# A hybrid attention and gMLP block: the output gate of the attention in pairs of products, one activation table, and the second branch's blocks beside two heads

## The chip, the core and the metric

The kernel runs on one core of one Trainium2 chip. It is written by hand in the Tile language: the program names tiles, pools and engines, and a scheduler orders the instructions of each engine. The metric is the device time of one execution in microseconds (us), here the median of three runs: 1114.92 us (1113.07, 1114.92 and 1116.30). Beside them stands one execution that the hardware profiler took.

## The reference, cut to what matters

One layer on 1024 tokens of 1024 features, fp32. There are four heads with keys of 128 and values of 256.

```python
h = rmsnorm(x, norm_g) * (1 + scale) + shift
p = h @ w_in                                  # 1024 x 8224
q, k, v, z_gla, ra_f, ra_b, u, vs, z_gmlp, m_gla, m_gmlp = split(p)
log_a = max(log_sigmoid(ra @ alpha_w + alpha_b) / 16, -1.25)      # one for each direction
o = gla(q, k, v, log_a_f) + flip(gla(flip(q), flip(k), flip(v), flip(log_a_b), strict))
o = o * rsqrt(mean(o * o) + eps) * gla_norm_g                     # for each head
y_gla = (o * silu(z_gla)) @ w_br_gla
vs = layernorm(gelu(vs)) * ln_g + ln_b
sg = einsum(gmlp_ws, vs) + gmlp_bs                                # chunks of 128 tokens
y_gmlp = (gelu(u) * sg * silu(z_gmlp)) @ w_br_gmlp
merged = sigmoid(m_gla) * y_gla + sigmoid(m_gmlp) * y_gmlp
return rmsnorm(x + gate * (merged @ w_out), final_g)
```

`gla` is a linear attention with a decay, in chunks of 64 tokens: with b the running sum of log_a inside a chunk, it takes q·exp(b) against k·exp(-b) under a triangular mask, and carries a state of 128x256 from chunk to chunk.

## The kernel before, in words

**Products.** Each fp32 operand is split into a high and a low part of the type fp32r: ACT casts the value to the high part and DVE subtracts that from the value (`split_w`, L174 and L175). A product is then three: high x high, high x low and low x high. `dense_fm` computes one block of 128 output columns for all 1024 tokens: 2 halves x 8 k-blocks x 3 = 48 products of 128x512 (L192 to L194). `dense_v` does the same with tokens on the partitions and 256 columns (L509 to L511).

**Pairs of seven products.** `pair(ba, bb, evac)` computes two such blocks at once. It takes sums of the weights (on POOL) and sums of quarters of h (the tiles T1 to T4, made once), and needs seven products of 12 where the two blocks alone would need eight: 7 x 12 = 84 in place of 96 (L546 to L548). DVE adds the partial results and `evac` takes the four quarters of the result. In the kernel before, the pairs hold the two merge gates (`pair_m`, whose tanh goes to the DRAM tiles `tb_d` and `ta_d`) and u and z_gmlp (`pair_uz`, whose product u·sg·silu(z) goes to `gg_d`).

**Stages.** (1) Load x and the modulation, make h high and low. (2) The vs branch with its layernorm and spatial product. (3) v of heads 0 and 1 and the sums T1 to T4; v goes to DRAM. (4) The pairs. Before the last three of them stand `low_rank_weights` and `residual_gate`, which loads eight tiles `wg` and adds them with factors on DVE (L664). (5) The high halves of h are loaded again, q and k of head 0 are computed, and then the attention runs. (6) The gated output GO is multiplied by w_br_gla, merged, multiplied by w_out, and normalized.

**The attention** has 16 units: for each head the sequence backward half 1, backward half 0, forward half 0, forward half 1 (`SEQ`). `front` of a unit (function `gla_unit`) makes the decay: a product `pm` of ST and RT (L764), then on ACT Abs, Exp and Ln (L766 to L768), a DVE subtraction (L769) and a running sum (L773), Exp for the chunk ends, `qh` and `b` (L783, L789, L791), their products with q and k, and the score product `pm` L797. `body` makes the states: `gla_ops` transposes `kh` and splits `kh` and `qh` (L807 to L817), then for each of four tiles there is a state product `pk` (L821 to L823), a DVE step that decays and adds the state, a cast on ACT and a subtraction on DVE (L844 and L845) that split it, and a product `po` of q with the state, evacuated to `op`. The forward units add the masked scores, the mean square, a power on POOL (L220), a scaling (L917), a transpose (L922) and the product with the gate tile `zg` and with `gn`.

**What fills the units.** The fronts and bodies are issued at a priority raised by 4000, so the scheduler puts the other work of the loop where they leave an engine free. That other work is dense blocks: v of head h+2, and q, k and z of head h+1, while head h runs (z of head 0 before the loop); beside head 3 the loads and splits of the second branch (`load_gg`) and its eight blocks `dense_yb`. `dense_z` computes silu(z) times two, as (1 + tanh(z/2))·z, from a tanh on ACT (L720) and a DVE step (L721); `gn` carries the factor 0.5. Tanh, Ln and the Exps need different activation tables; where ACT goes from one to another, an ACT_TABLE_LOAD stands ahead of the function.

**Queues and pools.** SP issues the weight loads, POOL's queue the loads and stores of v, g and the gates. `ht` is a pool of 30 tiles of 4 KB per partition, `w4` one of 12 such tiles, `w2` one of 16 of 2 KB and `w1` one of 8 of 1 KB. In PSUM there are three `pd`, two `pm`, two `po` and one `pk`.

## Time and profile before

| | before |
| --- | --- |
| median of 3 runs | 1114.92 us (1113.07 to 1116.30) |
| the profiled execution | 1113.34 us, of which the span is 1111.6 us |
| mean granted TensorE clock | 0.987 |
| TensorE (PE) busy | 1068.1 us |
| ACT busy | 462.8 us |
| POOL busy | 231.5 us |
| instructions in the span | 14297 |

The span is the time from the first to the last record of the trace, and it is what the shares refer to. PE is TensorE's product, PEld its weight load, which runs beside it; DVE is VectorE, ACT ScalarE, POOL GpSimd, SP the engine that issues most loads. A matmul's record is longer than what it occupies, since products are pipelined: the duration of one is read from a window that is full of them, by dividing. A group of instructions reads "line engine operation, output <- inputs by the program's names, count | busy us, mean ns of one | idle time of the engine just before them, and what ended most of it". A row of waits reads "who waited <- on whom, for what: total us, count, longest".

### The profile page before, as it was taken

To read this page: it belongs to the slowest core of one execution; us is meant where nothing else is said; L and a number is where in the kernel's file an instruction comes from. 1 tells how busy PE (TensorE), PEld (TensorE's weight loads), DVE (VectorE), ACT (ScalarE), POOL (GpSimd) and SP (SyncE) were. 2 spreads that over 40 slices of the span, in tenths; PEclk is the share of its full clock that TensorE was granted. 3 is DMA by queue.
4 is the path that set the end of the run, shared out by engine and by line. 5 is a ranking of instruction groups with operands and counts; after the bars stand their busy time and mean duration, and the time that the engine had idled before them with its cause. 6 is when DMAs were issued, how large, how long until landed. Compare 5 with 4: busy or idle time off the path is not lost.

```text
span 1111.6 us, 14297 instructions
## 1 busy us (share of the span) xinstructions
PE 1068.1 (96%) x5396; PEld 903.2 (81%) x5396; DVE 669.5 (60%) x1057; ACT 462.8 (42%) x780; POOL 231.5 (21%) x262
## 2 busy tenths in 40 slices
PE   6989999999999999989999979998999999999997
PEld 4768899888787878877898879887878888888886
DVE  5765577347666665664566585557788745664422
ACT  4453234232333333333566563556775515221222
POOL 2210213424334252611000011002002010022410
PEclk9999999999999999999999989998999999999999
DMA  9532235233233323367322115103256357516012
GB/s 360 209 107 88 79 126 198 82 106 112 95 123 104 114 105 105 120 230 277 138 83 89 38 49 179 38 19 133 72 177 216 107 193 241 202 58 232 19 57 95
DMA packets 53143, 143.91 MB, mean 129 GB/s; under 512 B 6895, under 2 KB 15087, under 8 KB 53074
## 3 DMA queue, kind: packets, MB, share of 16 engines
q1 hardware_dynamic: 40898, 102.42, 26.2%
q0 software_dynamic: 12176, 40.58, 10.0%
q8 instruction: 42, 0.69, 0.2%
q14 instruction: 27, 0.22, 0.1%
HBM read 104.18 MB, written 38.80 MB: 129 GB/s over the span
## 4 chain that ended last, share of the span: by engine, by line
PE 82%; DVE 5%; ACT 4%; DMA 2%; issue 2%; POOL 1%; SPq 0%; POOLq 0%; ACTq 0%; DVEq 0%
PE pd L193 7%; PE pd L192 7%; PE pd L194 7%; PE pd L211 4%; PE pd L210 4%; PE pd L212 4%; PE po L546 3%; PE po L547 3%; PE po L548 3%; PE pd L510 3%; PE pd L511 3%; PE pd L509 3%; PE pd L1024 3%; PE pd L1026 3%; PE pd L1025 3%
## 5 line engine op out<-in xcount | busy, mean ns | idle before, releaser
L193 PE MATMUL pd<-hl,wh 128*128 128x512 f32 x256 | 100.3, 392 | 0.0
L192 PE MATMUL pd<-hh,wh 128*128 128x512 f32 x256 | 100.1, 392 | 0.0
L194 PE MATMUL pd<-hh,wl 128*128 128x512 f32 x256 | 100.1, 391 | 0.0
L510 PE MATMUL pd<-tvl,hh 128*128 128x256 f32 (+1 forms) x256 | 74.7, 292 | 2.2 <-DVE tvl L175 2.2
L220 POOL TENSOR_TENSOR r<-ms,nhalf 128x1 f32<-128x1 f32 (+1 forms) x24 | 21.8, 909 | 257.7 <-DVE ms L219 184.5
L509 PE MATMUL pd<-tvh,hh 128*128 128x256 f32 (+1 forms) x256 | 74.4, 293 | 0.3 <-ACT tvh L174 0.3
L511 PE MATMUL pd<-tvh,hl 128*128 128x256 f32 (+1 forms) x256 | 74.6, 292 | 0.0
L175 DVE TENSOR_TENSOR wl<-ws,wh 128x1024 fp32r<-128x1024 f32 x32 | 39.1, 1222 | 30.2 <-ACT wh L174 25.9
L174 ACT CAST wh<-ws 128x1024 fp32r<-128x1024 f32 x32 | 33.6, 1049 | 53.8 <-DMA ws<-in_wf 48.3
L192 PEld LDWEIGHTS pd<-hh,wh 128*128 128x128 f32 x256 | 48.1, 188 | 8.9
L194 PEld LDWEIGHTS pd<-hh,wl 128*128 128x128 f32 x256 | 48.1, 188 | 8.8
L193 PEld LDWEIGHTS pd<-hl,wh 128*128 128x128 f32 x256 | 48.1, 188 | 8.8
L548 PE MATMUL pd<-hh,al 128*128 128x512 f32 x128 | 50.3, 393 | 2.7 <-DVE al L175 2.7
L510 PEld LDWEIGHTS pd<-tvl,hh 128*128 128x128 f32 x256 | 50.0, 195 | 2.9 <-DVE tvl L175 2.7
L546 PE MATMUL pd<-hh,ah 128*128 128x512 f32 x128 | 50.4, 394 | 1.3 <-ACT ah L174 1.3
L193 PE MATMUL pd<-ggl,wh 128*128 128x512 f32 x128 | 50.3, 393 | 1.2 <-DVE ggl L175 1.2
L192 PE MATMUL pd<-ggh,wh 128*128 128x512 f32 x128 | 50.4, 395 | 0.0
L509 PEld LDWEIGHTS pd<-tvh,hh 128*128 128x128 f32 x256 | 49.8, 196 | 0.7 <-ACT tvh L174 0.6
L194 PE MATMUL pd<-ggh,wl 128*128 128x512 f32 x128 | 50.2, 392 | 0.0
L511 PEld LDWEIGHTS pd<-tvh,hl 128*128 128x128 f32 x256 | 50.1, 196 | 0.0
L547 PE MATMUL pd<-hl,ah 128*128 128x512 f32 x128 | 49.9, 390 | 0.0
L1024 PE MATMUL pd<-gh,wh 128*128 128x512 f32 x128 | 49.9, 390 | 0.0
(316 smaller groups left out, 3042.8 us busy)
## 6 DMA issues: line engine op xcount, KB each, us to landing
ws<-in_wf SPq DMA_DIRECT2D x32, 512.0 KB, 3.8
ws<-in_wt SPq DMA_DIRECT2D x22, 512.0 KB, 4.1
wa<-in_wada SPq DMA_DIRECT2D x16, 512.0 KB, 8.8
wa<-in_wf SPq DMA_DIRECT2D x16, 512.0 KB, 3.7
wb<-in_wf SPq DMA_DIRECT2D x16, 512.0 KB, 4.8
xn<-in_x SPq DMA_DIRECT2D x8, 512.0 KB, 8.7
sg_d<-sg POOLq DMA_DIRECT2D x16, 256.0 KB, 2.4
vh_d<-vh SPq DMA_DIRECT2D x32, 128.0 KB, 1.9
```

The lines of the kernel that those rows point to most:

```text
L192: TE.matmul(acc, lhsT=hi[:, k, :], rhs=x.hi(k, half), start=(k == 0), stop=False)
L193: TE.matmul(acc, lhsT=hi[:, k, :], rhs=x.lo(k, half), start=False, stop=False)
L194: TE.matmul(acc, lhsT=lo[:, k, :], rhs=x.hi(k, half), start=False, stop=(k == KC - 1))
L210: TE.matmul(acc, lhsT=xh, rhs=hi[:, k % 2, :], start=(k == 0), stop=False)
L211: TE.matmul(acc, lhsT=xh, rhs=lo[:, k % 2, :], start=False, stop=False)
L509: TE.matmul(acc, lhsT=H.hi_t(k, t), rhs=hi, start=(k == 0), stop=False)
L510: TE.matmul(acc, lhsT=H.hi_t(k, t), rhs=lo, start=False, stop=False)
L511: TE.matmul(acc, lhsT=H.lo_t(k, t), rhs=hi, start=False, stop=(k == KC - 1))
L546: TE.matmul(acc, lhsT=a, rhs=xh(k), start=(first and k == 0), stop=False, skip_group_check=not first)
L547: TE.matmul(acc, lhsT=a, rhs=xl(k), start=False, stop=False, skip_group_check=not first)
L548: TE.matmul(acc, lhsT=b, rhs=xh(k), start=False, stop=(k == 3), skip_group_check=not first)
L1024: TE.matmul(acc, lhsT=hi[:, k, :], rhs=GO.hi(k, half), start=(k == 0), stop=False)
```

## The change

Four things change.

- The eight blocks of z are computed as four pairs (`pair_z`) among the other pairs, with the same tanh and DVE step, and stored by POOL in a new DRAM tile `z_d`. `dense_z` is gone; `load_z` loads both tiles of a head from POOL's queue, beside the loads of v. The second `pair_m` on `FB_MA` stands ahead of `low_rank_weights` and `residual_gate` now.
- After the last tanh the activation table that holds both Exp and Ln is loaded by an explicit instruction.
- The filling work is spread anew: head 0 has v of head 2 and q, k of head 1; head 1 has v of head 3 and q, k of heads 2 and 3; head 2 has the second branch's loads and its blocks 0 to 3; head 3 has blocks 4 to 7.
- The tiles `ggf` and `tb` come from the pool `w4` instead of `ht`, and `dense_yb` writes its result into `tb`, so that the tile `yb` is gone.

```diff
@@ -72,6 +72,7 @@
     gg_d = dram("gg_d", [KC, P, T])
     ta_d = dram("ta_d", [KC, P, T])
     tb_d = dram("tb_d", [KC, P, T])
+    z_d = dram("z_d", [KC, P, T])
     b12_d = dram("b12_d", [4, P, 1024])
 
     v_d = [dram(f"v{n}_d", [HEADS, 2, P, 4 * 256]) for n in "hl"]
@@ -631,6 +632,17 @@
         pair(FB_U + 2 * i, FB_U + 2 * i + 1, ev_u)
         pair(FB_ZG + 2 * i, FB_ZG + 2 * i + 1, ev_z)
 
+    def pair_z(i):
+
+        def ev(b, half, acc):
+            z = w2([P, 512], F32, "z")
+            last_tanh[0] = S.activation(z, acc, AF.Tanh, scale=0.5)
+            V.scalar_tensor_tensor(out=z, in0=z, scalar=1.0, in1=acc, op0=ALU.add, op1=ALU.mult)
+            G.dma_start(z_d[2 * i + b, :, half * 512:half * 512 + 512], z)
+        pair(FB_Z + 2 * i, FB_Z + 2 * i + 1, ev)
+
+    last_tanh = [None]
+
     def low_rank_weights():
 
         sa, sr = ht([P, 1024], F32, "sa"), ht([P, 1024], F32R, "sr")
@@ -681,10 +693,18 @@
     pair_uz(2)
     pair_m(FB_MA, ta_d, 0)
     pair_uz(3)
+    pair_m(FB_MA, ta_d, 1)
     low_rank_weights()
     residual_gate()
-    for i in range(1, 4):
-        pair_m(FB_MA, ta_d, i)
+    pair_z(0)
+    pair_m(FB_MA, ta_d, 2)
+    pair_z(1)
+    pair_m(FB_MA, ta_d, 3)
+    pair_z(2)
+    pair_z(3)
+
+    with tc.issue_after(last_tanh[0].ins):
+        S.preload_act_table_set("natural_log_exp_and_others")
 
     for c in range(2):
         hi, lo = H.make(c, 1)
@@ -710,16 +730,10 @@
             S.copy(k_t[h][:, half * 512:half * 512 + 512], acc)
         dense_fm(FB_K + h, H, ev)
 
-    def dense_z(h):
+    def load_z(h):
         for j in range(2):
-            zt = ht([P, T], F32, "zg")
-            z_t[h][j] = zt
-
-            def ev(half, acc):
-                sl = slice(half * 512, half * 512 + 512)
-                S.activation(zt[:, sl], acc, AF.Tanh, scale=0.5)
-                V.scalar_tensor_tensor(out=zt[:, sl], in0=zt[:, sl], scalar=1.0, in1=acc, op0=ALU.add, op1=ALU.mult)
-            dense_fm(FB_Z + h * 2 + j, H, ev)
+            zt = z_t[h][j] = ht([P, T], F32, "zg")
+            G.dma_start(zt, z_d[2 * h + j])
 
     dense_q(0)
     dense_k(0)
@@ -929,7 +943,6 @@
     PRI = 4000
     with tc.high_priority(offset=PRI):
         front(0, 0)
-    dense_z(0)
 
     GG = Act("gg")
 
@@ -937,33 +950,41 @@
         for half in range(2):
             for c in range(KC // 2):
                 hi, lo = GG.make(c, half)
-                g = ht([P, 2, 512], F32, "ggf")
+                g = w4([P, 2, 512], F32, "ggf")
                 for i in range(2):
                     nc.sync.dma_start(g[:, i, :], gg_d[2 * c + i, :, half * 512:half * 512 + 512])
                 split_w(flat(g), flat(hi), flat(lo))
 
     def dense_yb(j):
-        tb, y = ht([P, T], F32, "tb"), ht([P, T], F32, "yb")
+        tb = w4([P, T], F32, "tb")
 
         def ev(half, acc):
-            sl = slice(half * 512, half * 512 + 512)
-            nc.sync.dma_start(tb[:, sl], tb_d[j, :, sl])
-            V.scalar_tensor_tensor(out=y[:, sl], in0=tb[:, sl], scalar=1.0, in1=acc, op0=ALU.add, op1=ALU.mult)
-            G.dma_start(y2_d[j, :, sl], y[:, sl])
+            t = tb[:, half * 512:half * 512 + 512]
+            nc.sync.dma_start(t, tb_d[j, :, half * 512:half * 512 + 512])
+            V.scalar_tensor_tensor(out=t, in0=t, scalar=1.0, in1=acc, op0=ALU.add, op1=ALU.mult)
+            G.dma_start(y2_d[j, :, half * 512:half * 512 + 512], t)
         dense_fm(FB_YB + j, GG, ev)
 
+    def dense_qk(h):
+        dense_q(h)
+        dense_k(h)
+
     for h in range(HEADS):
-        if h + 2 < HEADS:
+        if h < 2:
             dense_v(h + 2, ht)
-        if h + 1 < HEADS:
-            with tc.issue_after(last_pow[0].ins):
+        with tc.issue_after(last_pow[0].ins):
+            load_z(h)
+            if h + 1 < HEADS:
                 load_v(h + 1)
-            dense_q(h + 1)
-            dense_k(h + 1)
-            dense_z(h + 1)
+        if h == 0:
+            dense_qk(1)
+        elif h == 1:
+            dense_qk(2)
+            dense_qk(3)
         else:
-            load_gg()
-            for j in range(KC):
+            if h == 2:
+                load_gg()
+            for j in range(4 * (h - 2), 4 * (h - 2) + 4):
                 dense_yb(j)
         with tc.high_priority(offset=PRI):
             for u in range(4):
```

In the order that results, the engines' rows move as follows. In these rows the line is that of the kernel in question: in the attention a line of the kernel before is 14 lower than its counterpart after (L764 and L778, L822 and L836), and L175 has become L176.

TensorE, right behind the decay product of head 1's first unit, in the kernel before (`pd` with `hh`, `hl` is a product of a dense block of q, k or z; `po` is a product with the state):

```order
L764 MATMUL pm_5819<-RT_4137,ST 128x512
L194 MATMUL pd_4745<-hh_106,wl_4715 128x512
L822 MATMUL po_5024<-sl_5021,qth_4974 128x256
L823 MATMUL po_5024<-sh_5020,qtl_4975 128x256
L192 MATMUL pd_4745<-hh_106,wh_4714 128x512
L193 MATMUL pd_4745<-hl_107,wh_4714 128x512
L194 MATMUL pd_4745<-hh_106,wl_4715 128x512
L192 MATMUL pd_4779<-hh_92,wh_4775 128x512
L193 MATMUL pd_4779<-hl_93,wh_4775 128x512
L194 MATMUL pd_4779<-hh_92,wl_4776 128x512
```

TensorE at the same place in the kernel after (`pk` is a state product):

```order
L778 MATMUL pm_5339<-RT_4687,ST 128x512
L836 MATMUL po_5229<-sl_5226,qth_5184 128x256
L837 MATMUL po_5229<-sh_5225,qtl_5185 128x256
L835 MATMUL pk_5294<-vh_4702,keh_5279 128x256
L836 MATMUL pk_5294<-vl_4703,keh_5279 128x256
L837 MATMUL pk_5294<-vh_4702,kel_5280 128x256
L835 MATMUL po_5289<-sh_5240,qth_5284 128x256
L836 MATMUL po_5289<-sl_5241,qth_5284 128x256
L837 MATMUL po_5289<-sh_5240,qtl_5285 128x256
L835 MATMUL pk_5309<-vh_4702,keh_5279 128x256
```

The dense products that stood between the state products are gone from this place; the state products follow each other.

ACT in the third unit of head 0, before (`vh` is the cast of a block of v that is evacuated):

```order
L766 ACTIVATE e_4936<-pm_4934 128x512
L767 ACTIVATE e_4936<-e_4936 128x512
L768 ACT_TABLE_LOAD
L768 ACTIVATE e_4936<-e_4936 128x512
L500 CAST vh_4486<-pd_4461 128x256
L783 ACT_TABLE_LOAD
L783 ACTIVATE e_842_4946<-c_841_4944 128x8
L789 ACTIVATE qh_4951<-b_4942 128x512
L500 CAST vh_4517<-pd_4492 128x256
L791 ACTIVATE b_4942<-b_4942 128x512
```

ACT in the same unit, after (`sh` is the cast of a state, `q` an evacuation):

```order
L780 ACTIVATE e_5246<-pm_5244 128x512
L781 ACTIVATE e_5246<-e_5246 128x512
L782 ACTIVATE e_5246<-e_5246 128x512
L858 CAST sh_5195<-s_5193 128x256
L723 ACTIVATE q_5025<-pd_5058 128x512
L797 ACTIVATE e_904_5256<-c_903_5254 128x8
L803 ACTIVATE qh_5261<-b_5252 128x512
L805 ACTIVATE b_5252<-b_5252 128x512
```

The two table loads, ahead of Ln and ahead of the next Exp, are gone. In the whole attention 33 stand before, and a single one, ahead of the attention, stands after.

DVE between the score products of units 3 and 4 (the decay factors, state splits L845, weight splits L175 and a gate product L721), before:

```order
L804 TENSOR_TENSOR b_5181<-b_5181,e_912_5185 128x512
L813 TENSOR_TENSOR qh_5190<-qh_5190,e_912_5185 128x512
L845 TENSOR_TENSOR sl_5021<-s_5018,sh_5020 128x256
L811 TENSOR_TENSOR kel_5210<-pm_5204,keh_5209 128x512
L838 COPY s_5088<-pk_5084 128x256
L845 TENSOR_TENSOR sl_5091<-s_5088,sh_5090 128x256
L817 TENSOR_TENSOR qtl_5215<-qh_5046,qth_5214 128x512
L911 TENSOR_TENSOR op_4978<-po_5078,op_4978 128x256
L175 TENSOR_TENSOR wl_5642<-ws_5639,wh_5641 128x1024
L721 SCALAR_TENSOR_TENSOR zg_4711<-zg_4711,pd_4745 128x512
L840 SCALAR_TENSOR_TENSOR s_5107<-s_5088,dec_4948,pk_5103 128x256
```

DVE at the same place, after:

```order
L818 TENSOR_TENSOR b_5347<-b_5347,e_934_5351 128x512
L827 TENSOR_TENSOR qh_5356<-qh_5356,e_934_5351 128x512
L176 TENSOR_TENSOR wl_5956<-ws_5953,wh_5955 128x1024
L825 TENSOR_TENSOR kel_5375<-pm_5369,keh_5374 128x512
L831 TENSOR_TENSOR qtl_5380<-qh_5261,qth_5379 128x512
L909 TENSOR_TENSOR atl_5384<-atb_5170,ath_5383 128x512
L176 TENSOR_TENSOR wl_6015<-ws_6012,wh_6014 128x1024
L852 COPY s_5398<-pk_5394 128x256
L925 TENSOR_TENSOR op_5288<-po_5388,op_5288 128x256
```

The gate's product is gone, and two weight splits (L176, those of k of head 2 and q of head 3) stand between the unit's own steps where one stood.

## Prediction

> **What bounds the kernel now.** I read the page's busy shares first, then the 40 slices, then cut the attention into stretches.
>
> ```profile
> PE 1068.1 (96%) x5396; PEld 903.2 (81%) x5396; DVE 669.5 (60%) x1057; ACT 462.8 (42%) x780; POOL 231.5 (21%) x262
> PE   6989999999999999989999979998999999999997
> PEclk9999999999999999999999989998999999999999
> 213.00:260.00 47.00, 47.00 (x208) 38.68 (x206) 21.86 (x24) 16.73 (x23) 19.75 (x20) 1.00 0.24 86
> ```
>
> TensorE is busy for 96% of the span, so the kernel is bound by the number of its products, except where slices 24 and 28 dip. The fourth row is a window over the pairs (columns: window, length, busy time and count of PE, weight loads, DVE, ACT, POOL, granted clock, DMA share, GB/s): 208 products of 512 columns in 47.00 us, or 0.226 us each, with DVE and POOL under half busy.
>
> The dips lie in the attention. It has 16 units (four heads, two directions, two halves). I call the score product L797 of unit k A(k), for k from 0 to 15, and the time from one to the next a stretch. The windows below run from A to A.
>
> ```profile
> 598.50:616.80 18.30, 18.30 (x96) 15.62 (x95) 11.77 (x23) 12.28 (x21) 0.00 (x0) 1.00 0.03 10
> 616.80:650.80 34.00, 30.75 (x178) 27.02 (x176) 22.37 (x47) 19.23 (x38) 1.48 (x1) 0.95 0.13 47
> 650.80:667.10 16.30, 12.85 (x82) 11.80 (x83) 13.33 (x28) 11.40 (x24) 2.36 (x3) 0.79 0.15 54
> 667.10:682.30 15.20, 15.20 (x129) 15.16 (x128) 10.84 (x20) 8.23 (x15) 3.28 (x6) 1.00 0.65 192
> ...
> 751.90:769.50 17.60, 13.43 (x82) 11.89 (x81) 12.73 (x31) 11.31 (x25) 4.50 (x7) 0.91 0.26 99
> 769.50:787.40 17.90, 17.27 (x85) 14.68 (x84) 13.11 (x25) 13.28 (x25) 1.10 (x2) 0.90 0.39 135
> ...
> 808.10:834.20 26.10, 23.72 (x120) 18.77 (x119) 23.55 (x42) 21.44 (x37) 2.18 (x3) 1.00 0.47 165
> ...
> sum 391.90, PE 378.01 PEld 329.20 DVE 258.79 ACT 222.28 POOL 30.51; mean PE 22.24 PEld 19.36 DVE 15.22 ACT 13.08 POOL 1.79
> ```
>
> Where TensorE has 15 us or more of products spread between two A, it is busy throughout (the first and the fourth row: 129 products, nearly all of 256 columns, in 15.20 us, 0.118 us each). Where it has about 10 us, 82 products in the third and fifth row, the stretch still takes 16 to 18 us: the unit's chain ends last there, not TensorE. The two long rows that are not full have a place of their own, the second head's v weights (34.00) and the second branch's loads (26.10). The five rows that are not full lose 3.25, 3.45, 4.17, 0.63 and 2.38 us idle and, by (1 - clock) x length, 1.7, 3.4, 1.6, 1.8 and 0 us to the clock. That makes **22.4 us lost in the attention**.
>
> **The change, part by part.** *Products.* Eight gate blocks of 48 products become four pairs of 84: 384 - 336 = 48 fewer, at 0.226 us: **-10.9 us**, all on the engine that bounds. What a gate pair adds elsewhere is hidden by its own 84 x 0.226 = 19.0 us of products: by the counts of one pair, DVE has 4 splits, 5 sums and 4 gate products, about 10.5 us, and ACT about 7.5 us.
>
> ```profile
> 487.88 1.28 DVE L664 SCALAR_TENSOR_TENSOR gacc<-wg,gsc,gacc 128x1024 f32<-128x1024 f32 x1 [2.82 <-DMA wg<-in_wgate]
> PE po L546 <- DVE u L593: 1.4, 1, 1.4
> ```
>
> The gate vector's eight loads now stand on SP between the weight loads of the later pairs, and DVE's sums over them stand among the pairs' evacuations; the rows show DVE held 2.82 us by one such load, and TensorE 1.4 us behind it. Five more of them would be 0 to 7 us. I take 0, since one of the seven sums, the one in that row, held TensorE before, and keep 7 for a rival.
>
> *Table loads.*
>
> ```profile
> L768 ACT ACT_TABLE_LOAD x16 | 20.5, 1283 | 0.3
> L783 ACT ACT_TABLE_LOAD x13 | 16.7, 1283 | 0.2
> L720 ACT ACT_TABLE_LOAD x3 | 3.8, 1283 | 0.1
> ...
> 655.68 1.28 ACT L768 ACT_TABLE_LOAD   x1
> 656.97 0.63 ACT L768 ACTIVATE e<-e 128x512 f32<-128x512 f32 x1
> 657.64 0.69 DVE L769 SCALAR_TENSOR_TENSOR e<-pm,e 128x512 f32<-128x512 f32 x1 [1.11 <-ACT e L768]
> ```
>
> With one at L767 these are 33 loads; the order of the changed kernel has one ahead of the attention. So 32 x 1.283 = 41 us of ACT go, but only those on a chain that ends last are worth anything, that is up to two in each bare stretch: the last three rows show one ahead of Ln and DVE waiting for it. Elsewhere TensorE's products hide them. The Trainium skill (page "ScalarE: Activation LUTs", section "What ACT_TABLE_LOAD costs") puts a further drain of 1.38 us on each switch, 2.66 us in all, which would free 85 us. The trace agrees with the load's 1283 ns but shows the next activation 1.29 us after the load's start, so no drain.
>
> *Cover.* This is the price of the change.
>
> ```profile
> 553.52 0.89 PE pm L797 x8
> ```
>
> Before, gate and q/k blocks stood between the units of heads 0 and 1; now the gate is gone from there, and the order leaves these products between one A and the next (counts of the order, 512 columns at 0.226, 256 at 0.118, an A with its transposes 1.3 by the row ahead): A2 to A3 8.2 us (18 before), A3 to A4 14.1 (18), A4 to A5 6.3 (28), A5 to A6 15.7 (10). From A6 on there are 15 to 26 us in each.
>
> How long does a bare stretch take? DVE's work between two A is nearest to it.
>
> ```profile
> L175 DVE TENSOR_TENSOR wl<-ws,wh 128x1024 fp32r<-128x1024 f32 x22 | 26.9, 1221 | 10.5 <-ACT wh L174 9.9 <-PE pd L193 0.6
> L845 DVE TENSOR_TENSOR sl<-s,sh 128x256 fp32r<-128x256 f32 x56 | 23.5, 420 | 10.3 <-ACT sh L844 10.2
> L769 DVE SCALAR_TENSOR_TENSOR e<-pm,e 128x512 f32<-128x512 f32 x16 | 11.1, 691 | 32.0 <-ACT e L768 31.9
> L917 DVE TENSOR_SCALAR op<-op,r 128x256 f32<-128x256 f32 x32 | 9.1, 349 | 3.1 <-POOL r L220 3.1
> L773 DVE TENSOR_TENSOR_SCAN b<-smask,e 128x512 f32<-128x512 f32 x8 | 9.8, 1219 | 0.1
> L867 DVE COPY_PREDICATED atb<-fmask,pm 64x512 f32<-64x512 int8 x8 | 5.8, 729 | 5.6 <-PE pm L797 5.5
> ```
>
> From DVE's order, counted from one product b L792 to the next and priced with such rows (1.22 for a split or a scan, 0.69 for 512 columns, 0.42 for 256 or less): A3 to A4 has 6 splits 7.3, a scan 1.2, 8 x 0.69 = 5.5, 15 x 0.43 = 6.5, one masked copy and small ones 1.1, so 21.6 us. In the same way A2 to A3 has 13.4, A4 to A5 14.9, A5 to A6 12.6. The same count for the three barest stretches of before gives 14.3, 15.5 and 14.7 against 16.3, 17.6 and 17.9 measured: 2.0 to 3.2 us more, with two table loads in each. If both were on the chain, a stretch will take its DVE work with nothing added (2.4 - 2.6); if one was, 1.1 more; if none, up to 3.2. I take 0.5. The losses are then 13.9 - 8.2 = 5.7, 22.1 - 14.1 = 8.0, 15.4 - 6.3 = 9.1, and none in the fourth: **22.8 us**.
>
> Two later stretches are short of cover too. A9 to A10, where the second branch's splits now fall, has 29.4 us of DVE work on 22.1 of products; A14 to A15 has 20.6 on 14.6. Ahead of both TensorE has more work than DVE (25.7 against 19.4, 18.2 against 12.6), so DVE can run ahead: each lies between 0 and about 8 or 6 us, and I take the middle, 4 and 3. Behind A15 37.6 us of products (55.3 before) stand beside 39.7 us of DVE work, of which the last 1.5 follow TensorE's last transposes: 1 us.
>
> ```profile
> 801.93 5.77 DMA ggf<-gg_d
> ```
>
> The second branch's loads cost a wait before too, this row on the chain of work that ended last. They now stand on SP ahead of the first block's weights, whose cast stands on ACT ahead of the state casts of unit 7, and whatever waits there holds the states and then TensorE. Nearest row 5.77 us, so 0 to 6; I take 0, as the loads' slots come free while q and k of head 3 still run. The 24 loads and stores of z on POOL are paid by an engine with 30.5 us of work in the 391.9. That ggf and tb move to pool w costs nothing as long as its 12 tiles hold two blocks' weights (3 each) beside them; a block that comes too late would be one more of these 5.77 us.
>
> **Sum** on the profiled execution (1113.34 us; span 1111.6): -10.9 for products, +22.8 + 4 + 3 + 1 = 30.8 lost in place of 22.4, so -10.9 + 8.4 = **-2.5 us**. That is 1110.8 from the profiled time and 1112.4 from the median shown, 1114.92; I say **1111 us**. A measurement of this kernel can tell about 0.3%, 3.3 us, from no change, so the forecast stands close to that edge.
>
> **The rivals.** *The loads were all on the chain and DVE runs ahead.* Then a bare stretch adds nothing (-0.5 each on three), and the later ones cost nothing (-8): 9.5 us less, **1102**. For it: the 1.11 us in which DVE waited for Ln behind a load. Against it: A9 to A10's DVE work exceeds its products by 7.3 us.
>
> *Slower: a bare stretch is set by round trips.* State, cast, subtraction and product follow one another across DVE, ACT and TensorE, and the loads stood in gaps of ACT, which is under 75% busy there. Then the 2.0 to 3.2 us stay: at 3.2 five stretches cost 2.7 more each, 13.5 us. Add that the 36 v products ahead of A4 wait for their second weights, whose tile, as I read the pool, is freed only by unit 2:
>
> ```profile
> PE pd L510 <- DVE tvl L175: 2.2, 2, 1.8
> ```
>
> this wait of 1.8 us stood there before as well, and 36 x 0.118 = 4.2 us at half clock are 4.2 more. That gives up to 1111 + 13.5 + 4.2 = 1129, and **1120** in its middle. It decides from 1.2 us added to each of the five (-2.5 + 5.8 is slower by 0.3%), that is from a stretch 1.7 us above its DVE work. The clock belongs to it: the row of 0.79 shows half rate after waits of less than 2 us. The Trainium skill (page "TensorE: Matmul & The Clock Gate", part 1) has the array fall to half rate by windows of about 3.4 us of activity, re-throttled some 5 us after the last matmul, and so speaks against a change that bares TensorE; the trace shows such a dip after much shorter waits. By that page one window in each of three stretches would be about 5 us more where TensorE is the limit.
>
> *The pairs give part back.* The gate loads stall five more evacuations, 7 us: **1118**.
>
> *The one table does not hold*: 32 loads stay, and the bare stretches take 2 us more each: 1117. The order shows a single load.
>
> **How the numbers follow.** Forecast (1105 to 1117) 0.50; all loads on the chain (below 1105) 0.17; round trips (above 1118) 0.22; pairs 0.09; table 0.02. Of the forecast's 0.50 I put 0.26 below 1111.6, so faster is 0.26 + 0.17 = 0.43; slower 0.22 and a third of the pairs, 0.25; same 0.32. The range runs from inside the fast rival, 1100, to inside the slow one, 1123, and leaves out some 0.1 on either side.
>
> **What would show it.** The pairs as one window: 0.226 us a product, and no loss above that around the gate loads. No ACT_TABLE_LOAD between the first and the last Exp. A2 to A3, A3 to A4 and A4 to A5 at 13.9, 22.1 and 15.4 us, with TensorE idle and a clock under 1.00 there; A6 to A9 full. If the three take their DVE work and no more, the fast rival holds; if they take 3 us more than it, the slow one. The prediction is wrong altogether if TensorE is idle at a place that I left at nothing: behind the second branch's loads, or after A15.

## The result: 1.2% slower, and the profile after

| | before | after |
| --- | --- | --- |
| median of 4 runs | 1114.61 us | 1127.72 us (1126.39 to 1132.89) |
| ratio | | 1.0121, 95% interval 1.0089 to 1.0154 |
| the profiled execution | 1113.34 us, span 1111.6 us | 1132.89 us, span 1131.2 us |

The change made the kernel slower by 13 us where 4 us less were forecast, outside the range of 1100 to 1123. The profiled execution of the changed kernel is the longest of its four runs, 5 us above their median; a second one of the same kernel (c1 below) took 1128.47 us, and where the two differ both are given. One run of e4 below was disturbed (3716.63 us) and stays out of e4's numbers.

The page's busy shares and its slices, after:

```profile
PE 1077.1 (95%) x5348; PEld 902.6 (80%) x5348; DVE 695.1 (61%) x1085; ACT 431.3 (38%) x760; POOL 264.3 (23%) x302
PE   6889999999999999999999988999899998999997
PEclk9999999999999999999999989999899997999999
```

TensorE has 48 products fewer, as forecast, and yet 9 us more of busy time. A slice is 28 us. In the attention the slices 24, 25, 29 and 34 are below 9 (24 and 28 before), and the clock dips in 24, 29 and 34.

The windows from A to A of the kernel after (A2 to A5, A8 to A10, A14 to A15, and from A15 to the last transposes; columns as in the prediction):

```profile
661.70:676.60 14.90, 11.59 (x58) 8.80 (x57) 11.92 (x25) 8.68 (x21) 0.00 (x0) 0.88 0.12 36
676.60:698.80 22.20, 19.61 (x119) 17.95 (x120) 20.59 (x38) 13.05 (x28) 1.04 (x1) 0.85 0.07 25
698.80:711.70 12.90, 9.96 (x57) 7.83 (x55) 11.66 (x25) 8.61 (x23) 1.17 (x2) 0.87 0.12 47
...
763.60:792.10 28.50, 26.95 (x156) 22.99 (x154) 16.71 (x39) 12.74 (x31) 2.23 (x3) 1.00 0.25 88
792.10:825.70 33.60, 28.73 (x123) 22.30 (x123) 27.07 (x47) 20.42 (x37) 6.28 (x10) 0.85 0.58 216
...
907.40:923.20 15.80, 15.34 (x89) 13.09 (x87) 15.10 (x28) 9.47 (x20) 2.17 (x4) 1.00 0.59 208
923.20:974.40 51.20, 45.73 (x214) 37.65 (x215) 33.28 (x63) 20.10 (x43) 2.04 (x2) 0.87 0.47 161
```

The first three rows are the stretches that the prediction called bare, at 14.9, 22.2 and 12.9 us (forecast 13.9, 22.1 and 15.4). The stretches between A5 and A8 and between A10 and A14 are full. The surprise stands in the fifth row and in the last: 33.6 us where 26 were forecast, and 51.2 where 38.6 were.

From here on **loss** is what lies between the starts of successive products beyond what a product of that form takes back to back (0.227 us for 512 columns, 0.118 to 0.12 for 256, 0.11 for 128). The four products that close the gate vector are counted at 0.43 us each, the time between their starts. For a window that holds 512-column products only the loss is read off directly, to within some 0.5 us. The pairs around the gate vector, before and then after:

```profile
460.00:530.00 70.00, 66.52 (x286) 53.20 (x285) 36.63 (x47) 25.45 (x34) 17.68 (x27) 1.00 0.66 241
```

```profile
460.00:530.00 70.00, 62.59 (x253) 48.92 (x252) 41.29 (x43) 26.21 (x34) 24.38 (x25) 0.95 0.51 171
```

286 products x 0.227 are 64.9 us of the 70, so some 5 are lost; 253 are 57.4, so 12.6 are lost. By the whole trace:

| loss, us | before | forecast of the change | after | again (c1) |
| --- | --- | --- | --- | --- |
| pairs, 460 to 530 | 4.9 | as before | 12.4 | 11.8 |
| A2 to A5 | 6.1 | 22.8 | 21.5 | 19.8 |
| A5 to A8 | 7.1 | 0 | 0.3 | 0.4 |
| A8 to A10 | 6.1 | 4 | 14.3 | 13.2 |
| A10 to A15 | 8.5 | 3 | 2.0 | 2.0 |
| behind A15 | 0.3 | 1 | 13.9 | 12.2 |

The 48 products less are 10.9 us, the pairs lose 7.5 us more and the attention 23.8 more (52.1 in place of 28.3, with A0 to A2): 20.4 us. The two spans differ by 19.6, so the rest of the traces differs by 0.8 us in sum.

### The profile page after: what moved, and what is told of

It is laid out like the page before. It is cut to its first block, busy times and chain, and to the rows that moved or that the text cites. A ratio compares the mean times of both kernels' runs of the same rounds, so it can differ in the third digit from the quotient of the medians.

```text
span 1131.2 us, 14327 instructions
## 1 busy us (share of the span) xinstructions
PE 1077.1 (95%) x5348; PEld 902.6 (80%) x5348; DVE 695.1 (61%) x1085; ACT 431.3 (38%) x760; POOL 264.3 (23%) x302
## 3 DMA queue, kind: packets, MB, share of 16 engines
q0 software_dynamic: 14608, 48.97, 11.8%
## 4 chain that ended last, share of the span: by engine, by line
PE 78%; DVE 7%; DMA 5%; ACT 3%; issue 2%; POOL 1%; SPq 0%; POOLq 0%; ACTq 0%; DVEq 0%
PE pd L193 5%; PE pd L194 5%; PE pd L195 5%; PE po L547 4%; PE po L548 4%; PE pd L211 4%; PE pd L212 4%; PE po L549 4%; PE pd L213 4%; PE pd L549 3%; PE pd L548 3%; PE pd L547 3%; PE pk L547 3%; PE pd L511 3%; PE pd L512 3%; PE pk L548 3%
## 5 line engine op out<-in xcount | busy, mean ns | idle before, releaser
L221 POOL TENSOR_TENSOR r<-ms,nhalf 128x1 f32<-128x1 f32 (+1 forms) x24 | 20.8, 866 | 236.4 <-DVE ms L220 234.2
L549 PE MATMUL pd<-hh,al 128*128 128x512 f32 x160 | 63.9, 399 | 3.1 <-DVE al L176 3.1
L548 PE MATMUL pd<-hl,ah 128*128 128x512 f32 x160 | 62.9, 393 | 0.0
L570 POOL TENSOR_TENSOR wsum<-wb 128x512 f32<-128x512 f32 x20 | 26.2, 1311 | 121.5 <-DMA wb<-in_wf 108.3
L176 DVE TENSOR_TENSOR al<-wa,ah 128x1024 fp32r<-128x1024 f32 x20 | 47.2, 2360 | 10.6 <-PE po L548 6.8
L193 PE MATMUL pd<-ggh,wh 128*128 128x512 f32 x128 | 51.5, 402 | 1.4 <-ACT wh L175 1.0
L1046 PE MATMUL pd<-gh,wl 128*128 128x512 f32 x128 | 50.7, 396 | 0.8 <-DVE wl L176 0.8
L193 PE MATMUL pd<-hh,wh 128*128 128x512 f32 x128 | 50.2, 392 | 0.0
L194 PE MATMUL pd<-hl,wh 128*128 128x512 f32 x128 | 50.2, 392 | 0.0
L195 PE MATMUL pd<-hh,wl 128*128 128x512 f32 x128 | 50.1, 391 | 0.0
L1047 PE MATMUL pd<-gl,wh 128*128 128x512 f32 x128 | 48.9, 392 | 0.0
L212 PE MATMUL pd<-tl,mh 128*128 128x512 f32 x120 | 46.9, 391 | 0.0
```

Source lines behind the costliest of these rows:

```text
L193: TE.matmul(acc, lhsT=hi[:, k, :], rhs=x.hi(k, half), start=(k == 0), stop=False)
L194: TE.matmul(acc, lhsT=hi[:, k, :], rhs=x.lo(k, half), start=False, stop=False)
L195: TE.matmul(acc, lhsT=lo[:, k, :], rhs=x.hi(k, half), start=False, stop=(k == KC - 1))
L212: TE.matmul(acc, lhsT=xh, rhs=lo[:, k % 2, :], start=False, stop=False)
L548: TE.matmul(acc, lhsT=a, rhs=xl(k), start=False, stop=False, skip_group_check=not first)
L549: TE.matmul(acc, lhsT=b, rhs=xh(k), start=False, stop=(k == 3), skip_group_check=not first)
```

## The experiments

Each ran on a chip together with the kernel before, so the ratios (with their 95% intervals) are what compares across chips; where two runs shared a chip their medians compare too. c1, e5, e6, e7, e8, e9 and e10 had one chip, e1 to e4 another, e11 and e12 a third, e13 a fourth.

| run | median, us | ratio to before | loss: pairs | A2 to A5 | A5 to A8 | A8 to A10 | A10 to A15 | behind A15 |
| --- | --- | --- | --- | --- | --- | --- | --- | --- |
| c1, the change again | 1130.74 | 1.0145 (1.0101 to 1.0189) | 11.8 | 19.8 | 0.4 | 13.2 | 2.0 | 12.2 |
| e1, gate vector last | 1142.59 | 1.0248 (1.0205 to 1.0291) | 7.5, and 19.7 ahead of A0 | 19.7 | 0.4 | 12.6 | 2.3 | 9.0 |
| e2, pool of 30 | 1130.34 | 1.0133 (1.0101 to 1.0166) | 12.1 | 21.4 | 0.4 | 14.6 | 9.1 | 0.5 |
| e3, late casts | 1130.92 | 1.0153 (1.0108 to 1.0198) | 11.5 | 20.8 | 2.6 | 14.9 | 2.1 | 8.7 |
| e4, no table | three runs, 1135.52 to 1142.61 | 1.0213 (1.0166 to 1.0259) | 9.4 | 27.6 | 1.9 | 14.3 | 2.1 | 10.1 |
| e5, q and k early | 1120.30 | 1.0046 (1.0022 to 1.0070) | 9.9 | 5.1 | 1.6 | 21.0 | 1.2 | 7.7 |
| e6, gate at old place | 1129.98 | 1.0133 (1.0101 to 1.0164) | 13.3 | 21.4 | 0.4 | 15.0 | 2.2 | 9.5 |
| e7, e5 and e6 | 1121.54 | 1.0045 (1.0024 to 1.0067) | 12.4 | 5.1 | 1.7 | 20.2 | 1.0 | 7.0 |
| e8, gate in halves | 1123.98 | 1.0086 (1.0059 to 1.0112) | 12.2 | 21.9 | 0.4 | 12.5 | 0.8 | 6.9 |
| e9, other spread | 1124.87 | 1.0073 (1.0049 to 1.0097) | 13.7 | 0.5 | 13.2 | 16.4 | 1.9 | 8.7 |
| e10, e5, e8 and e3 | 1126.69 | 1.0100 (1.0072 to 1.0128) | 12.6 | 5.1 | 1.6 | 21.2 | 4.6 | 8.8 |
| e11, small casts late | 1125.33 | 1.0115 (1.0084 to 1.0145) | 3.0, and 4.4 ahead of A0 | 21.1 | 0.4 | 17.5 | 2.0 | 10.1 |
| e12, e11 and e5 | 1115.71 | 1.0016 (0.9991 to 1.0040) | 2.5, and 5.3 ahead of A0 | 5.1 | 1.7 | 20.0 | 2.5 | 10.1 |
| e13, e12 and e2 | 1118.76 | 1.0042 (1.0027 to 1.0058) | 2.7, and 4.5 ahead of A0 | 5.2 | 1.6 | 24.8 | 9.1 | 0.9 |

### First theory: an engine stands at a late load

The chain of work that ended last, after (start, us, what), has three waits for weight loads in the attention:

```profile
787.12 5.64 DMA ws<-in_wf
...
805.60 9.79 DMA ws<-in_wf
...
934.29 6.96 DMA ws<-in_wf
941.33 1.06 ACT wh L175
942.42 1.23 DVE wl L176
```

And DVE around the third, in order of time (start, us, engine, line, what, idle time and what ended it):

```profile
942.42 1.23 DVE L176 TENSOR_TENSOR wl<-ws,wh 128x1024 fp32r<-128x1024 f32 x1 [6.79 <-ACT wh L175]
943.56 0.47 DVE L854 SCALAR_TENSOR_TENSOR s<-s,dec,pk 128x256 f32<-128x256 f32 x1
```

ACT stood at the cast `wh` of a weight whose load SP issued late, DVE stood 6.79 us for that cast, and the state step `s` of the last unit came behind the subtraction, at 943.56 us. The state product `pk` that it needs had ended at 939.5, so the state came 4.0 us late. Together with the gate loads this made the first theory: late loads, held by slots and by the order on SP, cost the three places. Three edits took them away, and a fourth took the table.

e1, the gate vector behind the last pair:

```diff
     low_rank_weights()
-    residual_gate()
     pair_z(0)
...
     pair_z(3)
+    with tc.issue_after(last_z[0].ins):
+        residual_gate()
```

> The change with the gate vector's sums put behind the last pair (the weights wg pass one at a time, since their pool has one slot left there; seven sums on DVE wait for them between the pairs' evacuations). Theory: DVE held by these loads holds TensorE; in the changed kernel's profile the pairs between 460 and 520 us lose 12.2 us against back-to-back products (4.6 us in the kernel before). Behind the last pair they hold nothing: the loss there falls under 4 us and the time falls by 7 to 9 us, to about 1119. Rival: the sums hold the evacuations of the first q and k blocks instead, and the time stays within 3 us of 1127.7.

It became slower by 1% more. In the waits of TensorE behind the pairs one row says it all:

```profile
PE pm L682 <- DVE gacc L676: 16.1, 1, 16.1
```

The eight loads still pass one after the other, and now the product that closes the gate vector, and all behind it on TensorE, waits for the last. In the pairs a loss of 7.5 us stayed although no gate sum stood there. So the gate sums were not all of it.

e2, the tiles of the second branch from the pool of 30:

```diff
-                g = w4([P, 2, 512], F32, "ggf")
+                g = ht([P, 2, 512], F32, "ggf")
...
-        tb = w4([P, T], F32, "tb")
+        tb = ht([P, T], F32, "tb")
```

> The change with the tiles ggf and tb taken from the pool of 30 again instead of the pool of 12. Theory: SP's loads of weights stand behind the loads of ggf and tb, which wait for slots of the pool of 12; the casts of those weights on ACT (waits of 5.64 and 9.79 us on the chain) hold the state casts behind them. With the other pool both waits go, the two stretches from A8 to A10 (28.5 + 33.6 us in the changed kernel) fall to about 51 us, and the time by 8 to 11 us, to about 1118. Rival: DVE's work (29.4 us between A9 and A10) is the limit there: that stretch stays above 29 us and the time within 4 us of 1127.7. The wait of 6.96 us behind A15 is not touched by either.

Its windows from A8 to A11, and behind A15:

```profile
765.20:795.30 30.10, 27.93 (x150) 24.18 (x150) 19.29 (x42) 14.73 (x34) 1.65 (x2) 0.92 0.27 89
795.30:813.20 17.90, 12.97 (x67) 10.58 (x66) 15.11 (x35) 11.58 (x29) 5.96 (x10) 0.84 0.44 169
813.20:829.10 15.90, 12.80 (x53) 9.78 (x54) 13.81 (x24) 9.49 (x19) 0.00 (x0) 0.79 0.66 238
916.00:970.50 54.50, 54.50 (x290) 46.65 (x290) 36.22 (x68) 19.36 (x42) 4.21 (x6) 1.00 0.56 185
```

A9 to A10 fell from 33.6 to 17.9 us and the end is full, and still the time stayed. The second branch's blocks now start later: A9 to A11 have 67 and 53 products where they had 123 and 106, and the products that left are the ones that fill the end. The waits for `ws` there are gone from the chain of work that ended last (one of 7.48 us for `ggf` stands in it), but with them gone TensorE had no other products to do there. The loss from A8 to the end went from 30.2 (c1: 27.4) to 24.2 us only.

e3, the fourth and later weight casts of w_br_gla behind the last state cast:

```diff
     for j in range(3, KC):
-        ya_w[j] = fm_weights(FB_YA + j)
+        with tc.issue_after(last_cast[0].ins):
+            ya_w[j] = fm_weights(FB_YA + j)
```

> The change with the casts of the fourth and later weight blocks of w_br_gla queued on ACT behind the last state cast. Theory: behind A15 ACT stands at such a cast for a weight that arrives 7 us late (6.96 us on the chain), and the last unit's states stand behind it; with the cast moved, A15 to the last transposes falls from 51 us to about 41 and the time by 6 to 9 us, to about 1120. Rival: the last unit's own chain across DVE, ACT and TensorE sets it (33 us of DVE work there), or the blocks that come later are missed as cover: the time stays within 3 us of 1127.7.

The end fell from 51.5 (c1: 49.8) to 45.1 us, but the tail behind it grew from 156.5 to 158.5, and the median stayed at 1130.92. So the late cast is worth some 3 to 4 us of the 12 to 14 lost there. DVE's row of the same state step says why it is no more:

```profile
939.30 0.48 DVE L854 SCALAR_TENSOR_TENSOR s<-s,dec,pk 128x256 f32<-128x256 f32 x1 [3.94 <-PE pk L837]
```

The state step came 4.3 us earlier (939.30 for 943.56), and now DVE stood 3.94 us for the state product itself, which follows some 5 us of dense products in TensorE's order; the next state step waited 1.89 us in the same way.

e4, without the explicit table load:

```diff
-    with tc.issue_after(last_tanh[0].ins):
-        S.preload_act_table_set("natural_log_exp_and_others")
```

> The change without the explicit table load: the attention has 33 table loads of 1.283 us again, ahead of each Ln and each following Exp (16 units x 2, and one). Theory of the prediction: only loads in stretches without cover count, and about 0.5 to 1.1 us of the two in each: with some seven such stretches the time rises by 3 to 8 us, to about 1133. Rival one: all loads there are on the chain, 2 x 1.283 x 7 = 18 us: about 1146. Rival two: all are hidden by other waits: within 2 us of 1127.7.

Its windows from A2 to A5:

```profile
660.30:677.80 17.50, 11.63 (x58) 8.82 (x57) 12.03 (x25) 11.22 (x22) 0.00 (x0) 0.84 0.09 31
677.80:701.20 23.40, 20.11 (x118) 18.32 (x119) 20.59 (x38) 15.54 (x30) 1.04 (x1) 0.83 0.07 23
701.20:716.40 15.20, 10.73 (x57) 8.39 (x55) 11.72 (x25) 10.97 (x24) 1.17 (x2) 0.78 0.11 43
```

17.5 in place of 14.9 and 15.2 in place of 12.9: 2.6 and 2.3 us, nearly the whole of two loads (2 x 1.283 = 2.57). The middle one, A3 to A4, takes 1.2 us longer (2.7 longer than in c1). Where no products cover the unit, both loads stand on its chain; where they do (A5 to A9, A10 to A15) a stretch stays within 1.6 us of what it was. Between the ratios of e4 and c1 lie 0.7%, 8 us, with intervals that just overlap. The Trainium skill (page "ScalarE: Activation LUTs", section "What ACT_TABLE_LOAD costs") has 1.28 us for the load, which agrees, and 1.38 us of drain on each switch, which the 2.6 and 2.3 us here do not bear out. By the page's figures two switches with their drains would be, as an estimate, 5.3 us in each of these stretches.

### Second theory: cover

What e2 showed made the second theory. A stretch from A to A takes 13 to 22 us even where few products stand in it, by the unit's own chain; TensorE loses what its products fall short of that, and a wait that goes is worth something only where other products stand ready. Then where the blocks are put matters more than any one wait.

c1 is the changed kernel again, as the measure on this chip.

> The changed kernel as it is, so that the others of this call have it on the same chip. Both theories: 1.1 to 1.6% slower than the kernel before.

e5, q and k of head 2 beside head 0:

```diff
         if h == 0:
             dense_qk(1)
+            dense_qk(2)
         elif h == 1:
-            dense_qk(2)
             dense_qk(3)
```

> The change with q and k of head 2 beside head 0 instead of head 1. Theory (cover): a stretch between two score products takes 13 to 22 us whatever stands in it, since the unit's own steps on DVE, ACT and TensorE follow one another; TensorE loses what its products fall short of that. By this kernel's order the products in A2 to A3 rise from 8 to 17 us, A3 to A4 from 14 to 15, A4 to A5 from 6 to 10.5, and A8 to A9 fall from 26 to 10. The loss of 21.5 us in the three bare stretches falls to about 8 to 11, A8 to A9 gets a new one of 3 to 5; the time falls by 7 to 11 us against the changed kernel. Rival (the blocks only move and the loss moves along with them, as it did with the pool): the time stays within 3 us of the changed kernel's.

Its windows from A2 to A5 and from A8 to A10:

```profile
663.20:681.20 18.00, 18.00 (x97) 15.40 (x96) 10.97 (x21) 8.75 (x18) 0.00 (x0) 1.00 0.00 1
681.20:697.20 16.00, 16.00 (x91) 13.91 (x90) 13.34 (x25) 9.94 (x22) 0.00 (x0) 1.00 0.10 34
697.20:712.80 15.60, 12.46 (x95) 11.14 (x93) 15.15 (x35) 9.92 (x24) 2.65 (x3) 1.00 0.06 24
765.80:787.20 21.40, 16.46 (x92) 14.06 (x92) 18.38 (x46) 13.32 (x36) 2.24 (x3) 0.78 0.22 75
787.20:819.80 32.60, 28.37 (x122) 22.11 (x122) 26.81 (x42) 18.18 (x30) 6.54 (x11) 0.88 0.65 234
```

The first two are full, the third loses 4.7. A2 to A5 lost 5.1 us in place of 19.8, A8 to A10 21.0 in place of 13.2, and the median fell by 10.4 us on the same chip. Nothing was taken away but the place of two blocks. The time fell as far as the theory had it (7 to 11 us). Of its parts, A2 to A5 lost less than expected (5.1 for 8 to 11) and A8 to A9, left with 10.5 us of products, far more (10.8 for 3 to 5): DVE is busy for 18.4 of its 21.4 us there.

e6, the gate vector back at its old place, and e7, both:

```diff
+    low_rank_weights()
+    residual_gate()
     pair_m(FB_MA, ta_d, 1)
-    low_rank_weights()
-    residual_gate()
```

> The change with the gate vector back ahead of the second pair on FB_MA, right behind the last pair of u and z_gmlp, where it stood before. Theory: the loss between 460 and 530 us, 12.4 us in the changed kernel and 4.9 in the kernel before, depends on what frees slots for the wg loads; at the old place it is about 5 again and the time falls by 6 to 8 us against the changed kernel. Rival: the pairs of z, which follow now where q and k blocks followed, are what makes it dearer (more evacuations on DVE behind each load); the loss stays above 10 us and the time within 2 us.

> Both edits (q and k of head 2 beside head 0, and the gate vector at its old place). If both theories hold the gains add: 13 to 19 us less than the changed kernel, which is the kernel before's time or up to 6 us below it. If the rivals hold: within 4 us of the changed kernel.

The place did nothing (loss 13.3, time within 1 us of c1), and e7 stands where e5 does. e8 gave the gate's weights more slots:

```diff
-            wg = ht([P, D], F32, "wg")
-            nc.sync.dma_start(wg, wgate[k])
...
+            for b in range(2):
+                wg = w2([P, 512], F32, "wg")
+                nc.sync.dma_start(wg, wgate[k, :, sl])
```

> The change with the gate vector's weights loaded as sixteen halves of 128x512 in the pool of sixteen 2 KB tiles, instead of eight tiles wg in the pool of 30, which has one slot left there. Theory (one slot: load, sum and next load follow one another, and DVE waits for each load between the pairs' evacuations): with several slots the halves arrive together and the loss between 460 and 530 us falls from 12 us to 5 or less; the time by 6 to 8 us against the changed kernel on this chip (1130.7), as far as the order of the attention stays. Rival: the sums themselves on DVE are what holds the evacuations, whatever the slots: the loss there stays above 10 us.

The loss in the pairs stayed (12.2), so one slot was not it either. The time fell by 7 us all the same, out of the attention: the edit had moved the order there (A4 to A5 now has 11.8 us of products, and the second branch starts otherwise), which says how much this part hangs on the spread. TensorE's longest wait between 455 and 530 us in this run:

```profile
PE pd L547 <- ACT ah L175: 4.3, 1, 4.3
```

In the changed kernel the same wait is shorter, and two for DVE are longer:

```profile
PE po L547 <- DVE u L594: 3.5, 2, 2.7
PE pd L549 <- DVE al L176: 2.3, 2, 1.6
PE pd L547 <- ACT ah L175: 1.6, 1, 1.6
```

ACT's rows ahead of that wait, in the changed kernel:

```profile
465.00 1.05 ACT L654 CAST sr<-sa 128x1024 fp32r<-128x1024 f32 x1 [2.04 <-DMA sa<-in_abias]
466.08 1.05 ACT L655 CAST ST<-sr 64x1024 fp32r<-64x1024 f32 x1
467.34 1.05 ACT L657 CAST ST<-sa 32x1024 fp32r<-32x1024 f32 x1 [0.21 <-DVE sa L656]
468.40 1.15 ACT L658 ACTIVATE sa<-sa,ident 32x1024 f32<-32x1024 f32 x1
469.57 1.04 ACT L175 CAST ah<-wa 128x1024 fp32r<-128x1024 f32 x1
```

ACT waits for the small low-rank weights and casts them in four steps, and the next pair's weight cast `ah` stands behind them. e11 keeps the halves of e8 and queues both, these casts and the gate's sums, behind work of a later pair, by when their loads have come (cut to the queueing):

```diff
     pair_z(0)
+    with tc.issue_after(last_tanh[0].ins):
+        low_rank_weights()
...
     pair_z(1)
+    with tc.issue_after(last_z[0].ins):
+        residual_gate()
```

> The change with the low-rank weights' casts on ACT behind the last tanh of the first pair of z, and the gate vector (in halves) with its sums on DVE behind the last step of the second pair of z; the attention's order is that of the changed kernel. Theory (ACT, in order, stands at the cast of sr for a load of 5 us, and the next pair's weight cast stands behind it; later DVE stands at the gate's loads): with both queued late enough that their loads have landed, the loss between 460 and 540 us falls from 12 us to under 5, and the time by 6 to 9 us against 1130.7, to about 1123. Rival (the extra work on ACT, DVE and POOL in this place is too much for the pairs, wherever it waits): the loss stays above 9 us.

> The same and q, k of head 2 beside head 0. If the gains add (10.4 us measured for the spread, 6 to 9 us for the gate): 1111 to 1115, the kernel before's time or a little below it. If the gate's loss stays: about 1120.

The same window of e11:

```profile
460.00:530.00 70.00, 68.24 (x297) 55.25 (x296) 39.39 (x41) 25.77 (x34) 29.32 (x32) 1.00 0.43 144
```

297 x 0.227 = 67.4 of 70: 2.6 lost in place of 12.6. Some of it comes back later (4.4 us ahead of A0, 1.3 in the changed kernel), and A0 stands 6.0 us earlier. The medians on different chips say 2 to 5 us; the ratio alone, 1.0115, does not tell it from the changed kernel's. Both edits together, e12, reach the kernel before: 1.0016 (0.9991 to 1.0040).

Two more spreads, e9 and e10, both with the edits of e3 and e8, and the pool of 30 on top of e12, e13 (their diffs are those above put together; e9 also moves k of head 3 to head 2, v of head 3 behind q of head 3 with its weights from the pool of 12, and one block of the second branch from head 2 to head 3):

> Three edits on the change: the gate's halves, the late weight casts behind the last state cast, and another spread: head 0 has v of head 2 and q, k of heads 1 and 2; head 1 has q of head 3 and v of head 3 (its weights from the pool of 12); head 2 has k of head 3, the second branch's loads and blocks 0 to 2; head 3 blocks 3 to 7. By its order the products between score products are 17, 17, 16 us in A2 to A5, then 8.4 and 10.7 (A5 to A7), 13 in A8 to A9 and 23 in A9 to A10. Theory (cover: a stretch takes 13 to 18 us at least): losses of 7 + 5 + 3 us there, none in A2 to A5, and if the second branch's loads find the products beside them none in A9 to A10; with 7 us from the gate about 1108 to 1114, no slower than the kernel before. Rival (the wait for the second branch's splits stays, 20 us in A8 to A10): 1120 or more.

> Three edits on the change: the gate's halves, the late weight casts behind the last state cast, and q, k of head 2 beside head 0. If the gains add: 7 us from the gate, 10.4 as measured with the spread alone, 3 from the casts: 1110 to 1114, the kernel before's time or a little below it. If the last unit's loss and the wait in A8 to A10 (20 us) only move: 1118 or more.

> The kernel of e12 with ggf and tb from the pool of 30 again. By its order the products between score products are 9.4, 8.6 and 13 us in A8 to A11 (10, 22 and 20 in e12) and 52 us behind A15 (37 in e12). Theory (cover): A8 to A11 cost 15 to 18 us each, so losses of about 6 + 8 + 3 us there and none behind A15, 17 us against some 30 in e12: the time falls by about 8 to 12 us, to 1104 to 1108, below the kernel before's. Rival (the loss only moves, as in e2): 1113 to 1118.

All three missed what the theory had for them; each came out where its rival had it or up to 1 us above. e9 fills A2 to A5 and bares A5 to A8, where it loses 13.2. e10 keeps the 5.1 us of e5 in A2 to A5, but its median stands 6.4 us above that of e5 on the same chip: what e3 and e8 changed are no terms that add. e13 repeats e2: its end is full, and A8 to A11 cost what that saves:

```profile
760.40:785.10 24.70, 18.75 (x86) 15.69 (x85) 22.53 (x49) 15.28 (x37) 2.23 (x3) 0.69 0.34 125
785.10:804.20 19.10, 14.69 (x68) 11.86 (x68) 15.19 (x31) 11.03 (x28) 5.33 (x9) 0.77 0.56 207
804.20:824.70 20.50, 18.14 (x77) 14.39 (x76) 15.73 (x25) 11.02 (x20) 0.00 (x0) 0.85 0.37 135
```

With 9.7, 9.0 and 13.5 us of products these three took 64 us where 48 were expected. The loss from A8 to the end was 34.8 us here and 32.6 in e12, and 24.2 in e2 and 30.2 (c1: 27.4) in the changed kernel: the pool mainly sets where it falls, and how much it is changes by a few us, up or down. No kernel here is faster than the kernel before.

## Why the prediction was wrong, step by step

**Products: right.** 48 fewer, and the pairs run at 0.227 us a product.

**Table loads: right that they count only where cover is short, too small there.** I took 0.5 us above DVE's work in a bare stretch, between the case of both loads on the chain and that of neither. e4 shows both on it. The rival's ground (all loads on the chain) was true; its result, 1102, was not, since its other half, that DVE runs ahead, failed.

**Bare stretches: right in sum, 22.8 us forecast and 21.5 measured.** Singly they were 5.7, 8.0 and 9.1 against 6.7, 8.1 and 6.7: DVE's work gave the sizes to within 2.5 us, and that the sum is closer than its parts is luck. e5 shows the mechanism: with products put there the loss goes.

**"I take 0, since one of the seven sums ... held TensorE before": wrong, 7.5 us, about the 7 that the rival had.** The mechanism was only in part the one priced. Taking away the sums (e1), the place (e6) or the slots (e8) did not bring the loss down to that of the kernel before. With ACT's casts of the small weights queued late together with the sums it fell to 3.0 (e11). The sums alone, taken out by e1, were worth 4 to 5 us of it; the casts alone were not moved in any run.

**"DVE can run ahead: each lies between 0 and about 8 or 6 us, and I take the middle": wrong for A9 to A10.** With A8 to A9 the loss was 14.3 us for the 4 forecast. The second branch's splits were not done ahead, as their rows in the changed kernel show (durations least, median and most in ns, then the first and last start):

```profile
L193 PE MATMUL pd<-ggh,wh x128: 387/390/796, 801.4 to 919.5; 128*128 128x512 f32 x128
...
L175 ACT CAST ggh<-ggf x8: 1040/1045/1057, 800.1 to 816.4; 128x1024 fp32r<-128x1024 f32 x8
L176 DVE TENSOR_TENSOR ggl<-ggf,ggh x8: 1206/1214/1221, 802.2 to 818.6; 128x1024 fp32r<-128x1024 f32 x8
```

All eight fall between 800 and 819 us. SP waited there (total us, count, longest):

```profile
SPq L955 <- PE pd L195: 26.1, 2, 13.5
```

The loads of `ggf` (L955) take slots of the pool of 12, and SP stood at them until products of the q and k blocks had freed some. The prediction let the move to that pool cost nothing, or one more wait of 5.77 us if the 12 tiles were short. The waits came (5.64 and 9.79 us on the chain), but e2, which undoes the move, brings no time all the same.

What is common to all runs is a gap at the hand-over. The last product on h started at 786.0 us and the first one on the second branch at 801.4, and between them TensorE had only the units' own products: 7.7 of the 14.3 us were lost there. In the kernel before the two started at 812.2 and 812.5, beside head 3, and A12 to A13 lost 4.4. In every experiment the gap is there, from 14.0 us (e1) to 36.1 (e13). I had priced the first block's load (0 to 6, taken at 0) and not the gap.

What makes the gap is not shown. The split tiles come from the pool of 30 that also holds h, so they could be waiting for h's room; but in e5 the last product on h started at 764.8 and the last load of `ggf` had landed by 769.3, and the first cast came only at 792.7, in ACT's order behind the steps of a unit.

**"Behind A15 ... 1 us": wrong, 13.9 (12.2).** The order gave 37.6 us of products beside 39.7 us of DVE work, and I took the two to run side by side. They did not: the last unit's states came 4 us late behind a weight's cast (6.96 us on the chain), with that cast moved they waited for state products behind dense ones (e3), and 6.7 us more went to the clock (last section). Before, four more blocks stood there, 55 us of products, and 0.3 us were lost. e2 and e13, which have 290 and 285 products there, lose 0.5 and 0.9. The prediction had named an idle TensorE at these last two places as what would show it wrong altogether, and both came.

**The kernel before lost more than I counted:** 28.3 us in the attention by the count used here, 22.4 by idle time and clock of five rows. That was a help of 6 us to the change, so the error of the steps was larger than the 22 us by which the profiled execution missed: 7.5 in the pairs, 10.3 in A8 to A10 and 12.9 behind A15, less 6 here and some 3 in other terms.

The forecast's rivals had 1118 for the pairs and 1120 for the round trips, up to 1129. The time came out near the upper end of the second, by another mechanism: not dearer bare stretches but the pairs and two more places without cover.

What stays open: how much of the pairs' loss the small casts alone carry, and what holds the second branch's splits back, so that 20 to 35 us are lost from A8 to the end in every run with the change where the kernel before loses 14.9. No run freed the room of h or moved the splits ahead in the order.

## What to carry to other kernels

Work taken out of a stretch is worth its time only if that stretch has more products than its chain needs: write down, from the order, the products between the steps of the recurrent chain and compare each with the engine that carries the chain. Look above all at hand-overs, where one set of blocks ends and the next needs loads and splits of its own first: here 14 to 36 us without a product of either stood between them. And a wait on the chain of work is not what its removal brings: e2 and e3 brought no time that can be told, with waits of 5 to 10 us gone.

## What the runs showed of the hardware that was not expected

After short waits TensorE's clock was low for far longer than they lasted. The changed kernel, around the wait behind A15:

```profile
942.00:946.00 4.00, 2.24 (x14) 1.59 (x13) 2.84 (x6) 2.32 (x6) 0.00 (x0) 1.00 0.00 0
946.00:959.50 13.50, 11.70 (x43) 9.62 (x42) 10.96 (x24) 5.95 (x16) 1.03 (x1) 0.50 0.80 263
```

After gaps of 1.65, 0.60 and 0.57 us the granted clock was 0.50 for 13.5 us, 6.7 us of the 13.9 lost there. Over the five windows of the kernel after that show a clock under 1.00, (1 - clock) x length gives 18.5 us beside 19.2 us of idle time. Not every gap has this behind it: the kernel before was idle for 2.38 us between 808.1 and 834.2 us at a clock of 1.00. The Trainium skill (page "TensorE: Matmul & The Clock Gate", part 1) has full rate return after about 3.4 us of sustained work; here TensorE's records cover 87% of those 13.5 us and the rate stayed at half.
